# All gate/up chunks of an encoder's feed-forward by seven products, with the two half-token products of a chunk run ahead of its other five

## The chip, the cores and the metric

The kernel runs on one core of one Trainium2 chip. The metric is the device time of one execution in microseconds (us); the comparison is of medians of several executions. The engines are named as in the profile: PE is TensorE's matmul, PEld its weight load, DVE the vector engine, ACT the scalar engine, POOL GpSimd, SP the engine that issues most transfers.

## What is computed

A two-layer bidirectional encoder on 512 tokens of width 1024, everything in float32. Each layer mixes tokens (attention heads and a short convolution side by side) and then runs a gated feed-forward of hidden width 2816:

```
for l in range(DEPTH):                                   # DEPTH = 2
    h = rms_norm(x, pre_mix_norm[l])
    ... attention heads and convolution -> merged ...
    mix = einsum('bse,ed->bsd', merged, w_out[l])
    x = x + rms_norm(mix, post_mix_norm[l])
    h = rms_norm(x, pre_ffn_norm[l])
    g, u = split(einsum('bsd,df->bsf', h, w_gate_up[l]), 2, axis=-1)
    f = einsum('bsf,fd->bsd', silu(g) * u, w_down[l])
    x = x + rms_norm(f, post_ffn_norm[l])
```

The change is in the line of `g, u`: a product of [512 x 1024] by [1024 x 5632].

## The kernel before

**Precision.** Every float32 operand A of a matmul is split into a high part (`hi`, A rounded to TensorE's fast float32 form, a cast on ACT) and a low part (`lo` = A - hi, a subtraction on DVE), and a product is three matmuls: hi*hi, hi*lo, lo*hi. So each block of 128 x 1024 weights costs a cast and a subtraction, beside its matmuls.

**Tiles.** Tokens are in four tiles of 128 (t = 0..3), the width 1024 in eight blocks of 128 (four make a group g = 0, 1). `hT[k][g]` holds the transposed, normalized activations: k = 0 high, k = 1 low, [128, 4, 512 tokens] each. `transposed(t, ...)` (lines 237 to 248) fills one token tile: eight transposes on PE into two PSUM banks, a cast on ACT (L245), a subtraction on DVE (L246), and for the feed-forward a plain copy on ACT (L248) into `raw`. The hidden width is 22 chunks (m = 0..21) of 128 gate and 128 up columns. A chunk's weights come as two transfers of 512 KB (`load_raw`, three buffers tagged `raw`), and are split in halves (`split_half`, L177 on ACT and L178 on DVE) into four buffers `wh`/`wl`.

**A chunk in the direct way** (`pair_full`, m = 0 to 3 before): 2 outputs x 8 blocks x 3 = 48 matmuls with 512 tokens as the moving side; m = 0 and 1 run in two halves of 256 tokens (2 x 48 matmuls), since the token tiles 2 and 3 are not there yet when gate/up starts.

**A chunk by seven products** (`seven`, m = 4 to 21 before): a scheme of Strassen's kind on the 2 x 2 blocks (gate/up columns by width groups on one side, width groups by token halves on the other). Each product is 4 blocks x 3 = 12 matmuls with 256 tokens, so a chunk is 84 of these. It needs sums of token halves (`make_sums`, once per layer, from `raw`: four sums, each then split in high and low) and, for each chunk, four sums of weight blocks (`prepare`: t1 to t4 by four subtractions on DVE, then the splits of t1, t2, of t3, t4 and of the plain blocks b11, b21, b22). Five products use the token sums or the second token half. Two (b11 and b21) use only the first 256 tokens: product b11 by `hT` group 0 and product b21 by group 1, one after the other into the same bank `x`, which after both holds the gate of the first 256 tokens and after the first starts the bank `y`.

**Order.** PE and SP run in the order in which the program writes their instructions (`manual_schedule`). ACT and DVE are put in order at compile time by a planner that goes by its own costs, and takes, of the instructions that it thinks are ready, the one that the program writes first. Each engine then runs its list in that fixed order and waits where an operand is not there.

**Around the change.** In `out_proj`, for each token tile t, the mix is read out of PSUM (`evac`, L660 to L664), its norm is worked out (`rsqrt_mean`), x is updated (`residual`, L629), and the tile is normalized for the feed-forward (`normed`, L232 to L234); tiles 0 and 1 are transposed inside `out_proj`, tiles 2 and 3 inside the first chunks of gate/up. After gate/up come the 22 x 2 blocks of the down product, whose operands are split by `split` (L693, L694).

Of the kernel before, what the change touches and what calls it, by code (L numbers as in the profile page):

```python
# [16 lines left out]
F32 = mybir.dt.float32  # L17
# [6 lines left out]
P = 128  # L24
# [16 lines left out]
NDIRECT = 2  # L41

SEVEN = 4
# [34 lines left out]
def encoder(ctx: ExitStack, tc: tile.TileContext, x, xT, pos, mask, cols, rows, w, out):  # L78
# [32 lines left out]
    def load_raw(i, c=0, d=1024):  # L111

        if i >= 2 * DEPTH * NCHUNK:
            return
# [7 lines left out]
    x_sb = [cpool.tile([P, D], F32, tag=f"x{t}", name=f"x{t}") for t in range(NT)]  # L122
# [45 lines left out]

    def split_half(i):
# [8 lines left out]
        nc.vector.tensor_sub(lo, raws[i], hi.bitcast(F32))  # L178

# [451 lines left out]
    def out_proj(l, merged, sq_a, sq_c, inv):  # L631
# [40 lines left out]
        for t in range(NT):  # L672
# [5 lines left out]
            hs[t] = normed(t, gffn)  # L678
        return hT, hs, raw

    def feed_forward(l, hT, hs, raw):
# [9 lines left out]
        def split(m, src):  # L691
            hi, lo = act_dst(m)
            nc.scalar.copy(hi, src)  # L693
            nc.vector.tensor_sub(lo, src, hi.bitcast(F32))  # L694

        def unsplit(m):

            i = m - NDIRECT
            if i < 8:
                key, make, k = i // 4, lambda: big([P, 4, S]), i % 4  # L700
            elif i < 12:
                key, make, k = i // 2, lambda: sb.tile([P, 2, S], F32, tag="gain", bufs=2, name=nm("gain")), i % 2
            elif i < 18:
                key, make, k = i // 2, lambda: mid([P, 2, S]), i % 2
            else:
                key, k = i, 0
                make = lambda: sb.tile([P, 1, S], F32, tag="u" if i == 18 else "sqa", bufs=1, name=nm("u"))
# [3 lines left out]

        def gated(m, gate, up):

            if m < NDIRECT:
                nc.vector.tensor_mul(gate, up, gate)
                split(m, gate)
            else:
                nc.vector.tensor_mul(unsplit(m), up, gate)

        def gated_full(m, accs):  # L720
            sg = tmp([P, S])
            nc.scalar.activation(sg, accs[0], AF.Silu)
            gated(m, sg, accs[1])

        def turning(t):
            n = [0]

            def step():
                n[0] += 1
                if n[0] == TURN_GU:  # L730
                    transposed(t, hs[t], hT, "att", raw)
            return step
# [6 lines left out]
        def quarter(tiles, g, f):  # L739
            return tiles[g][:, :, f * HS:f * HS + HS]  # L740

        def make_sums():
            a11, a12, a21, a22 = (quarter(raw, g, f) for g, f in ((0, 0), (1, 0), (0, 1), (1, 1)))
            for o, x, y, op, g, f in ((a22, a21, a22, ALU.add, 1, 1), (a21, a11, a21, ALU.subtract, 0, 1),
                                      (a11, a22, a11, ALU.subtract, 0, 0), (a12, a12, a11, ALU.subtract, 1, 0)):
                nc.vector.tensor_tensor(o, x, y, op)
                yield
# [3 lines left out]
                hi = quarter(sums[0], g, f)  # L751
                nc.scalar.copy(hi, o)
                yield
                nc.vector.tensor_sub(quarter(sums[1], g, f), o, hi.bitcast(F32))
                yield

        def split_pair(src, n=1024):
            hi = sb.tile([P, 1024], F32R, tag="wh", bufs=WBUFS, name=nm("wh"))
            lo = sb.tile([P, 1024], F32R, tag="wl", bufs=WBUFS, name=nm("wl"))
            for c in range(0, n, 512):  # L760
                nc.scalar.copy(hi[:, c:c + 512], src[:, c:c + 512])  # L761
            nc.vector.tensor_sub(lo[:, :n], src[:, :n], hi[:, :n].bitcast(F32))  # L762
            return [(hi[:, c:c + 512], lo[:, c:c + 512]) for c in range(0, n, 512)]

        made = {}

        def prepare(m):
# [4 lines left out]
            b1, b2 = raws[i], raws[i + 1]  # L772
            (b11, b12), (b21, b22) = ((b[:, :512], b[:, 512:]) for b in (b1, b2))
            t12 = sb.tile([P, 1024], F32, tag="kl", bufs=2, name=nm("t"))
            t34 = sb.tile([P, 1024], F32, tag="kl", bufs=2, name=nm("t"))
            load_raw(i + 2)
            ops["b11"], = split_pair(b1, 512)
# [4 lines left out]
            load_raw(i + 3)  # L782
            yield
            ops["t1"], ops["t2"] = split_pair(t12)
            yield
            nc.vector.tensor_sub(t34[:, 512:], b21, t12[:, 512:])
            yield
            ops["b21"], ops["b22"] = split_pair(b2)
            yield
            ops["t3"], ops["t4"] = split_pair(t34)  # L790
            yield

        def down_splits():
            for k in (0, None, 1, None, 2, None):
                if k is not None:
                    split_half(2 * (l * NCHUNK + 38) + k)
                yield

        def seven(m, y, ahead):


            ops = made.pop(m)
            x, q = bank("acc"), bank("acc")

            def product(o, weights, tiles, g, f, start):
                hi, lo = weights
                a, b = quarter(tiles[0], g, f), quarter(tiles[1], g, f)
                for k in range(4):
                    c = slice(k * P, k * P + P)
# [225 lines left out]
```

## Time and profile before

| | us |
|---|---|
| median of 3 executions | 1184.53 (1184.43 to 1184.53) |
| profiled execution, device time | 1181.35 |
| its span, first to last instruction | 1179.6 |
| PE busy | 1161.3 (98%) |
| DVE busy | 788.5 (67%) |
| ACT busy | 628.4 (53%) |
| gate/up of layer 0, first matmul to first matmul of down | 236.28 to 468.72 |

The span begins with the first instruction. "Busy" of PE includes the overlap of neighbouring matmuls, so the start-to-start distance of matmuls is the better measure of its work. A timeline row gives the start, the duration, the engine, the line, the operation, the output and inputs, and in brackets how long the engine sat idle before it and which instruction ended that. Durations of neighbours on ACT and DVE overlap by some hundredths of a microsecond too: the start-to-start distance is what one costs in a full queue. The two layers have the same pattern; layer 1 is shifted by 584.40 us.

### The profile page before, as it was taken

To read this page: it belongs to the slowest core of one execution; us is meant where nothing else is said; L and a number is where in the kernel's file an instruction comes from. 1 tells how busy PE (TensorE), PEld (TensorE's weight loads), DVE (VectorE), ACT (ScalarE), POOL (GpSimd) and SP (SyncE) were. 2 spreads that over 40 slices of the span, in tenths; PEclk is the share of its full clock that TensorE was granted. 3 is DMA by queue.
4 is the path that set the end of the run, shared out by engine and by line. 5 is a ranking of instruction groups with operands and counts; after the bars stand their busy time and mean duration, and the time that the engine had idled before them with its cause. 6 is when DMAs were issued, how large, how long until landed. Compare 5 with 4: busy or idle time off the path is not lost.

```text
span 1179.6 us, 17833 instructions
## 1 busy us (share of the span) xinstructions
PE 1161.3 (98%) x7000; PEld 1018.9 (86%) x7000; DVE 788.5 (67%) x1330; ACT 628.4 (53%) x1217; POOL 33.8 (3%) x55
## 2 busy tenths in 40 slices
PE   9999999989999999999999999999999999999997
PEld 7777778888999999888877777788899999998886
DVE  4798655786888888432557986458868888883323
ACT  7577544663565557331445775437636555582311
POOL 5000001000000000000000000100000000000000
PEclk9999999999999999999999999999999999999999
DMA  8221123123333333423132211322223333333221
GB/s 320 90 72 54 55 66 112 56 98 99 107 99 103 106 107 110 158 74 114 46 117 80 72 54 57 99 95 72 79 90 103 106 108 108 108 126 123 91 72 72
DMA packets 33205, 114.38 MB, mean 97 GB/s; under 512 B 3936, under 2 KB 3936, under 8 KB 33120
## 3 DMA queue, kind: packets, MB, share of 16 engines
q1 hardware_dynamic: 32400, 112.15, 29.1%
q8 instruction: 55, 0.90, 0.3%
q10 hardware_dynamic: 720, 1.09, 0.2%
q14 instruction: 30, 0.25, 0.1%
HBM read 111.12 MB, written 2.10 MB: 96 GB/s over the span
## 4 chain that ended last, share of the span: by engine, by line
PE 92%; DVE 4%; ACT 2%; issue 1%; DMA 0%; DVEq 0%; SPq 0%
PE acc L811 18%; PE att L811 13%; PE acc L190 13%; PE acc L192 13%; PE acc L191 13%; PE att L190 4%; PE att L192 4%; PE att L191 4%; PE pv L427 3%; PE att L420 2%; PE att L403 1%; PE att L404 1%; ACT mid L232 1%; PE pv L192 1%; PE pv L190 1%
## 5 line engine op out<-in xcount | busy, mean ns | idle before, releaser
L178 DVE TENSOR_TENSOR wl<-raw,wh 128x1024 fp32r<-128x1024 f32 x120 | 146.5, 1222 | 165.5 <-ACT wh L177 164.9
L177 ACT CAST wh<-raw 128x1024 fp32r<-128x1024 f32 x120 | 125.7, 1050 | 177.7 <-PE acc L192 67.4
L811 PE MATMUL acc<-big,wh 128*128 128x256 f32 x1152 | 212.0, 283 | 0.0
L190 PE MATMUL acc<-big,wh 128*128 128x512 f32 (+1 forms) x496 | 184.8, 372 | 0.0
L191 PE MATMUL acc<-big,wh 128*128 128x512 f32 (+1 forms) x496 | 180.1, 363 | 1.1 <-DVE big L246 1.1
L192 PE MATMUL acc<-big,wl 128*128 128x512 f32 (+1 forms) x496 | 180.1, 363 | 0.0
L811 PEld LDWEIGHTS acc<-big,wh 128*128 128x128 f32 x1152 | 179.8, 192 | 0.2
L811 PE MATMUL acc<-big,wl 128*128 128x256 f32 x576 | 163.0, 283 | 0.0
L811 PE MATMUL att<-big,wh 128*128 128x256 f32 x864 | 160.4, 283 | 0.0
L811 PEld LDWEIGHTS att<-big,wh 128*128 128x128 f32 x864 | 134.7, 192 | 0.2
L811 PE MATMUL att<-big,wl 128*128 128x256 f32 x432 | 122.3, 283 | 0.0
L762 DVE TENSOR_TENSOR wl<-t,wh 128x1024 fp32r<-128x1024 f32 x72 | 88.0, 1223 | 43.0 <-ACT wh L761 43.0
L761 ACT CAST wh<-t 128x512 fp32r<-128x512 f32 x144 | 88.7, 619 | 45.9 <-PE att L811 31.7
L811 PEld LDWEIGHTS acc<-big,wl 128*128 128x128 f32 x576 | 110.6, 192 | 0.0
L192 PEld LDWEIGHTS acc<-big,wl 128*128 128x128 f32 x496 | 93.6, 189 | 15.2
L190 PE MATMUL acc<-wh,big 128*128 128x512 f32 x272 | 106.4, 391 | 0.2 <-ACT wh L524 0.2
L191 PEld LDWEIGHTS acc<-big,wh 128*128 128x128 f32 x496 | 93.8, 189 | 14.5 <-DVE big L246 1.7
L191 PE MATMUL acc<-wl,big 128*128 128x512 f32 x272 | 106.1, 390 | 0.2 <-DVE wl L525 0.2
L192 PE MATMUL acc<-wh,big 128*128 128x512 f32 x272 | 105.9, 389 | 0.0
L190 PEld LDWEIGHTS acc<-big,wh 128*128 128x128 f32 x496 | 93.7, 189 | 13.7 <-issue 0.8
L190 PE MATMUL att<-wh,big 128*128 128x512 f32 x228 | 89.4, 392 | 0.0
L761 ACT CAST wh<-raw 128x512 fp32r<-128x512 f32 x108 | 63.4, 619 | 48.5 <-PE acc L811 31.3
(212 smaller groups left out, 1942.9 us busy)
## 6 DMA issues: line engine op xcount, KB each, us to landing
raw<-in_w SPq DMA_DIRECT2D x192, 512.0 KB, 3.7
gain<-in_rows SPq DMA_DIRECT2D x7, 512.0 KB, 5.6
big<-in_xT SPq DMA_DIRECT2D x8, 256.0 KB, 5.5
raw<-in_w SPq DMA_DIRECT2D x8, 256.0 KB, 5.5
x<-in_x SPq DMA_DIRECT2D x4, 512.0 KB, 7.0
out_dram<-x SPq DMA_DIRECT2D x4, 256.0 KB, 2.1
out_dram<-x ACTq DMA_DIRECT2D x4, 256.0 KB, 2.1
mask_sb<-in_mask SPq DMA_DIRECT2D x1, 448.0 KB, 7.7
```

The lines of the kernel that those rows point to most:

```text
L177: nc.scalar.copy(hi, raws[i])
L178: nc.vector.tensor_sub(lo, raws[i], hi.bitcast(F32))
L190: nc.tensor.matmul(o, sh, mh, start=start, stop=False)
L191: nc.tensor.matmul(o, sh, ml, start=False, stop=False)
L192: nc.tensor.matmul(o, sl, mh, start=False, stop=stop)
L232: nc.scalar.activation(h[:, c], x_sb[t][:, c], AF.Square, accum_out=ss[:, f:f + 1])
L403: nc.tensor.matmul(sc, qk[:, hd, q0:q0 + P], qk[:, 2 + hd, :], start=True, stop=False)
L420: nc.tensor.transpose(tp[:, k * P:(k + 1) * P], sm[:, k * P:(k + 1) * P], ident)
L427: nc.tensor.matmul(o[hd * 64:hd * 64 + 64, half * 256:half * 256 + 256], V[:, k, hc:hc + 64], PT[hd][:, k, :], start=k == 0, stop=k == NT - 1)
L761: nc.scalar.copy(hi[:, c:c + 512], src[:, c:c + 512])
L762: nc.vector.tensor_sub(lo[:, :n], src[:, :n], hi[:, :n].bitcast(F32))
L811: nc.tensor.matmul(o[:, :HS], sh[:, c], mh[:, k, :], start=start and k == 0 and n == 0, stop=k == 3 and n == 2, skip_group_check=True)
```

## The change

All 22 chunks go by seven products. The order of the seven is changed: the two that need only the first half of the tokens (now called the lead of a chunk, `lead1` and `lead2`) are run ahead of the other five (`rest`). The first six leads of a layer (`LEAD` = 6) run one after another at the start of gate/up, each pair with a product of a neighbouring chunk in between, because the second adds to the bank that ACT reads after the first. Token tile 2 is transposed after the second lead's first product, token tile 3 after the fifth's, and each is followed by its part of the token sums (`make_sums(j)`, now by blocks of 128 tokens). The remaining 16 leads are spread over the 22 `rest`s, one in each of 16 of them. The first product of a lead leaves its result in the place where the chunk's output will stand (`unsplit`), from which the `rest` copies it into `y`. The last product (t4) of a chunk moves into the next chunk's `rest`, behind t2.

Lead weights are loaded apart (two transfers of 256 KB, the blocks b11 and b21), and split apart; the `rest` loads the whole chunk again for the four sums and b22. For the buffers of the leads from chunk 6 on, the four tiles of x (512 KB each) are written to DRAM by transfers of the POOL queue after `normed`, and read back after gate/up. Results of gate/up are all kept unsplit until the down product.

```diff
-NDIRECT = 2
-SEVEN = 4
+LEAD = 6
+TURN_LEAD = {1: 2, 4: 3}
...
     def split_half(i):
-        if i >= 2 * DEPTH * NCHUNK or i in halves or SEVEN <= i // 2 % NCHUNK - 16 < MT:
+        if i >= 2 * DEPTH * NCHUNK or i in halves:
             return
-        for k in range(i, min(i + RAW_AHEAD, 2 * DEPTH * NCHUNK - 1) + 1):
-            if k not in raws:
-                load_raw(k)
+        for k in range(i, i + RAW_AHEAD + 1):
+            load_ahead(k)
+        r = gate_half(i)
+        if r is not None:
+            if r < LEAD:
+                split_lead(i // (2 * NCHUNK), r)
+            return
...
+    def load_lead(l, m):
+        if (l, m) in lead_raws:
+            return
+        if m < LEAD:
+            r = sb.tile([P, 1024], F32, tag="raw", bufs=RAW_AHEAD + 1, name=nm("raw"))
+        else:
+            r = sb.tile([P, D], F32, tag="x", bufs=4, name=nm("raw"))
+        lead_raws[l, m] = r
+        for k in range(2):
+            nc.sync.dma_start(r[:, k * 512:k * 512 + 512], w[l * NCHUNK + 16 + m][:, k * 1024:k * 1024 + 512])
+
+    def split_lead(l, m):
+        if (l, m) not in leads:
+            leads[l, m] = split_pair(lead_raws[l, m], 1024, ("wh", "wl") if m < LEAD else ("x", "x"))
...
             hs[t] = normed(t, gffn)
+            nc.gpsimd.dma_start(x_away[:, t, :], x_sb[t])
...
-        def make_sums():
-            a11, a12, a21, a22 = (quarter(raw, g, f) for g, f in ((0, 0), (1, 0), (0, 1), (1, 1)))
+        def make_sums(j):
+            part = [[quarter(raw, g, f, j * P, P) for f in range(2)] for g in range(2)]
+            (a11, a21), (a12, a22) = part
             for o, x, y, op, g, f in ((a22, a21, a22, ALU.add, 1, 1), (a21, a11, a21, ALU.subtract, 0, 1),
                                       (a11, a22, a11, ALU.subtract, 0, 0), (a12, a12, a11, ALU.subtract, 1, 0)):
                 nc.vector.tensor_tensor(o, x, y, op)
+            for o, g, f in ((a22, 1, 1), (a11, 0, 0), (a21, 0, 1), (a12, 1, 0)):
...
-                hi = quarter(sums[0], g, f)
+                hi = quarter(sums[0], g, f, j * P, P)
                 nc.scalar.copy(hi, o)
-                nc.vector.tensor_sub(quarter(sums[1], g, f), o, hi.bitcast(F32))
+                nc.vector.tensor_sub(quarter(sums[1], g, f, j * P, P), o, hi.bitcast(F32))
...
         def prepare(m):
...
             nc.vector.tensor_sub(t12[:, :512], b12, b11)
             nc.vector.tensor_sub(t12[:, 512:], b22, t12[:, :512])
             yield
             nc.vector.tensor_sub(t34[:, :512], b22, b12)
+            load_rest(m + 1, 1)
+            nc.vector.tensor_sub(t34[:, 512:], b21, t12[:, 512:])
             ops["t1"], ops["t2"] = split_pair(t12)
             yield
             ops["t3"], ops["t4"] = split_pair(t34)
             yield
+            ops["b22"], = split_pair(b22, 512)
+            yield
...
+        def lead1(m):
+            x = firsts[m] = bank("acc")
+            product(x, leads[l, m][0], hT, 0, 0, True)
+            nc.scalar.copy(unsplit(m)[:, HS:], x[:, :HS])
+
+        def lead2(m):
+            x = firsts.pop(m)
+            product(x, leads[l, m][1], hT, 1, 0, False)
+            nc.scalar.activation(unsplit(m)[:, :HS], x[:, :HS], AF.Copy if m < LEAD else AF.Silu)
+
+        def last_product(m, y, up):
+            place = unsplit(m)
+            product(y, made.pop(m)["t4"], hT, 1, 1, False)
+            if m < LEAD:
+                nc.scalar.activation(place[:, :HS], place[:, :HS], AF.Silu)
+            nc.scalar.activation(place[:, HS:], y[:, :HS], AF.Silu)
+            nc.vector.tensor_mul(place, up, place)
+
+        def rest(m, y, before, ahead, led):
+            ops = made[m]
+            q = bank("acc")
             up = tmp([P, S])
             p5 = row([P, HS])
+            nc.scalar.copy(y[:, :HS], unsplit(m)[:, HS:])
             product(q, ops["t1"], sums, 1, 1, True)
             nc.scalar.copy(p5, q[:, :HS])
             next(ahead)
             product(y, ops["t2"], sums, 0, 0, False)
             nc.scalar.copy(up[:, :HS], y[:, :HS])
             next(ahead)
+            if before is not None:
+                last_product(*before)
             next(ahead)
+            if led is not None:
+                lead1(led)
             product(y, ops["t3"], sums, 0, 1, False)
             nc.scalar.copy(up[:, HS:], y[:, :HS])
+            nc.vector.tensor_add(up[:, HS:], up[:, HS:], p5)
             product(q, ops["b22"], sums, 1, 0, False)
             nc.vector.tensor_add(up[:, :HS], q[:, :HS], up[:, :HS])
+            if led is not None:
+                lead2(led)
             next(ahead)
+            return m, y, up
...
         ahead = None
+        for m in range(LEAD):
+            for k in range(m, min(m + 3, LEAD)):
+                load_lead(l, k)
+                split_lead(l, k)
+            if m + 3 < LEAD:
+                load_lead(l, m + 3)
+            lead1(m)
+            if m in TURN_LEAD:
+                t = TURN_LEAD[m]
+                transposed(t, hs[t], hT, "att", raw)
+            if m > 0:
+                lead2(m - 1)
+            if m in TURN_LEAD:
+                make_sums(t - 2)
+            if m == LEAD - 3:
+                ahead = prepare(0)
+            if ahead is not None:
+                next(ahead)
+        lead2(LEAD - 1)
         next(ahead)
...
+        led = LEAD
+        load_lead(l, led)
+        split_lead(l, led)
+        load_lead(l, led + 1)
+        before = None
+        for m in range(MT):
+            with_lead = led < MT and led < LEAD + (m + 1) * (MT - LEAD) // (MT - 1)
+            before = rest(m, ys[m % 2], before, prepare(m + 1) if m + 1 < MT else down_splits(),
+                          led if with_lead else None)
+            if with_lead:
+                led += 1
+                if led < MT:
+                    split_lead(l, led)
+                if led + 1 < MT:
+                    load_lead(l, led + 1)
+        last_product(*before)
+        for t in range(NT):
+            x_sb[t] = sb.tile([P, D], F32, tag="x", bufs=4, name=nm("x"))
+            nc.gpsimd.dma_start(x_sb[t], x_away[:, t, :])
```

More of the change, by code (lines that the diff above doesn't have):

```diff
@@ L750, in make_sums, with load_rest @@
                         sums[k][g] = big([P, 4, S], F32R)
-                hi = quarter(sums[0], g, f)
+                hi = quarter(sums[0], g, f, j * P, P)
                 nc.scalar.copy(hi, o)
-                yield
-                nc.vector.tensor_sub(quarter(sums[1], g, f), o, hi.bitcast(F32))
[L755 to L763, printed above, removed]
+                nc.vector.tensor_sub(quarter(sums[1], g, f, j * P, P), o, hi.bitcast(F32))
         made = {}
+        def load_rest(m, h):
+            if m < MT and 2 * (base + m) + h not in raws:
+                load_raw(2 * (base + m) + h)
         def prepare(m):
@@ L791, in prepare @@
             yield
[L793 to L809, printed above, removed]
-                    for n, (sh, mh) in enumerate(((hi, a), (hi, b), (lo, a))):
-                        nc.tensor.matmul(o[:, :HS], sh[:, c], mh[:, k, :], start=start and k == 0 and n == 0,
-                                         stop=k == 3 and n == 2, skip_group_check=True)
-            hA = [[hT[k][g] for g in range(2)] for k in range(2)]
+            ops["b22"], = split_pair(b22, 512)
@@ new lines, in prepare, with product @@
+            yield
+        def product(o, weights, tiles, g, f, start):
+            hi, lo = weights
+            a, b = quarter(tiles[0], g, f), quarter(tiles[1], g, f)
+            for k in range(4):
+                c = slice(k * P, k * P + P)
+                for n, (sh, mh) in enumerate(((hi, a), (hi, b), (lo, a))):
+                    nc.tensor.matmul(o[:, :HS], sh[:, c], mh[:, k, :], start=start and k == 0 and n == 0,
+                                     stop=k == 3 and n == 2, skip_group_check=True)
@@ L815, in seven @@
+        def rest(m, y, before, ahead, led):
+            ops = made[m]
+            q = bank("acc")
             up = tmp([P, S])
-            gate = tmp([P, S])
             p5 = row([P, HS])
-            product(x, ops["b11"], hA[0:2], 0, 0, True)
-            nc.scalar.copy(y[:, :HS], x[:, :HS])
-            next(ahead)
+            nc.scalar.copy(y[:, :HS], unsplit(m)[:, HS:])
             product(q, ops["t1"], sums, 1, 1, True)
@@ L887, in feed_forward @@
         hs = [None] * NT
-        done = set()
+        done = set(range(4))
         def down(f, m, t, acc, keep=None):
-            if m >= NDIRECT and m not in done:
-                split(m, unsplit(m))
+            if m not in done:
+                split(m)
             done.add(m)
@@ L913, in feed_forward @@
                     for k in range(m, min(m + 4, MT)):
-                        if k >= NDIRECT and k not in done:
-                            split(k, unsplit(k))
+                        if k not in done:
+                            split(k)
                             done.add(k)
-                    if m == 14 - 3:
+                    if m == 18 - 3:
                         gpost = load_row(l, 3)
```

128 lines of the change are left out of this document (47 added, 81 removed).

## The prediction, made before the changed kernel was run

> **What bounds the kernel now.** I read the page first, for the engine on which the end hangs.
>
> ```profile
> PE 1161.3 (98%) x7000; PEld 1018.9 (86%) x7000; DVE 788.5 (67%) x1330; ACT 628.4 (53%) x1217; POOL 33.8 (3%) x55
> ...
> PE 92%; DVE 4%; ACT 2%; issue 1%; DMA 0%; DVEq 0%; SPq 0%
> ```
>
> PE is busy for 98% of the span, and 92% of the chain of waits is PE. So a change pays by fewer or cheaper matmuls, as long as nobody makes PE wait. The next question is what stands still in the stage that is changed. The table of stretches (length in us, busy time of PE, PEld, DVE, ACT, POOL with instruction counts, granted clock, DMA share, GB/s) gives, for layer 0, the first four chunks and then the eighteen that already go by seven products:
>
> ```profile
> 236.28:287.29 51.01, 47.62 (x309) 43.33 (x308) 38.52 (x58) 27.02 (x50) 0.00 (x0) 1.00 0.31 103
> 287.29:468.73 181.44, 181.44 (x1514) 181.34 (x1513) 145.94 (x198) 110.22 (x239) 0.00 (x0) 1.00 0.33 105
> ```
>
> In the second stretch PE never stops. In the first it stands 51.01 - 47.62 = 3.39 us, and the waits of PE between 236 and 288 name them (engine, line, releaser, us, times, longest):
>
> ```profile
> PE att L241 <- DVE small L213: 2.8, 1, 2.8
> PE acc L191 <- DVE big L246: 0.5, 1, 0.5
> ```
>
> L241 is the transposing of token tile 2. It waits for DVE. How full DVE is there, the stretches show:
>
> ```profile
> 236.00:246.00 10.00, 6.61 (x52) 6.08 (x52) 9.93 (x22) 6.74 (x17) 0.00 (x0) 1.00 0.62 206
> 258.00:269.00 11.00, 11.00 (x78) 10.28 (x77) 10.97 (x12) 8.73 (x11) 0.00 (x0) 1.00 0.28 97
> 269.00:287.29 18.29, 18.29 (x83) 15.18 (x82) 9.59 (x13) 4.49 (x9) 0.00 (x0) 1.00 0.36 115
> ```
>
> DVE is full until 246 and again from 258 to 269 (tail of the output projection, then token sums and weight splits), and only then has slack. The four direct chunks are what gives it that time. This is the place where the change presses.
>
> **The change, part by part.** *Matmuls saved.* Start-to-start distances on PE (timeline rows; the two rows of the chain of waits are 84 matmuls apart):
>
> ```profile
> 236.28 0.28 PE L190 MATMUL acc<-big,wh 128*128 128x256 f32 x1
> 237.32 0.28 PE L192 MATMUL acc<-big,wl 128*128 128x256 f32 x1
> 237.44 0.28 PE L190 MATMUL acc<-big,wh 128*128 128x256 f32 x1
> 244.40 1.06 PE L241 MATMUL att<-ident,mid 128*128 128x128 f32 x8 [2.85 <-DVE small L213]
> 245.22 0.36 PE L190 MATMUL acc<-big,wh 128*128 128x256 f32 x1
> ...
> 287.29 2.87 PE acc L811 x24
> 297.37 2.88 PE acc L811 x24
> ...
> 275.32 0.60 ACT L722 ACTIVATE tmp<-acc 128x512 f32<-128x512 f32 x1 [4.32 <-PE acc L192]
> 286.20 0.60 ACT L722 ACTIVATE tmp<-acc 128x512 f32<-128x512 f32 x1 [3.80 <-PE acc L192]
> ...
> 468.72 0.40 PE L190 MATMUL acc<-wh,big 128*128 128x512 f32 x1
> ```
>
> A 256-token matmul costs 0.120 us (237.44 - 237.32), a chunk by seven products 297.37 - 287.29 = 10.08 us = 84 x 0.120, one product of twelve 1.44 us. A direct chunk costs 286.20 - 275.32 = 10.88 us, and one run in two token halves 96 x 0.120 = 11.52 us. The four direct chunks of a layer cost 2 x 11.52 + 2 x 10.88 = 44.80 us and become 40.32 us: 4.48 us less PE work a layer.
>
> The Trainium skill (TensorE: Matmul & The Clock Gate, "Wait — 56ns, not 53.3ns?") puts matmuls at N / 2.4 GHz plus about 2.5 ns, measured there on bf16: 109 ns for 256 columns and 216 for 512, by which the saving would be about 5.0 us a layer, an estimate. The trace has 120 ns and 10.88 / 48 = 227 ns, so it disagrees by some 11 ns on each, and the rows decide.
>
> *What DVE must do first.* Product t1 of a chunk needs split weight sums, and from the first chunk on it needs the token sums of all tiles. Before, the first such product ran at 287.29. Now it is the thirteenth product. I count it from where DVE has finished with the last token tile's normalization. The rows (DVE timeline; neighbours give what an instruction takes in a full queue):
>
> ```profile
> 249.10 1.28 DVE L234 SCALAR_TENSOR_TENSOR mid<-x,small,gain 128x1024 f32<-128x1024 f32 x1
> 252.32 1.29 DVE L246 TENSOR_TENSOR big<-att,big 128x512 fp32r<-128x512 f32 x2 [1.93 <-ACT big L245]
> ...
> 257.80 1.22 DVE L178 TENSOR_TENSOR wl<-raw,wh 128x1024 fp32r<-128x1024 f32 x1
> 258.94 2.48 DVE L746 TENSOR_TENSOR big<-big,big 128x1024 f32<-128x1024 f32 x2
> ...
> 273.16 0.69 DVE L781 TENSOR_TENSOR t<-raw,raw 128x512 f32<-128x512 f32 x1
> 273.76 0.68 DVE L786 TENSOR_TENSOR t<-raw,t 128x512 f32<-128x512 f32 x1
> ...
> 295.61 0.42 DVE L834 TENSOR_TENSOR tmp<-tmp,row 128x256 f32<-128x256 f32 x1
> 295.96 0.42 DVE L833 TENSOR_TENSOR tmp<-acc,tmp 128x256 f32<-128x256 f32 x1
> ```
>
> A subtraction of 1024 elements costs 258.94 - 257.80 = 1.14 us, one of 512 elements 0.60 (273.76 - 273.16), one of 256 0.35. L234 ends its share at 249.10 + 1.20 = 250.3. Up to there the work is the same as before, instruction for instruction (two lead splits of 1024 elements stand for two half-chunk splits). From 250.3 on, until PE can run t1 of chunk 1, the program has DVE do:
>
> - leads 4, 5 and 6, low parts: 3 x 1.14 = 3.42
> - token tile 3, low parts: 2 x 0.60 = 1.20
> - token sums in blocks of 512 elements: 2 tiles x (4 sums + 4 low parts) x 0.60 = 9.60
> - chunk 0: four weight sums 2.40, low parts of t1/t2 and t3/t4 2.28, of b22 0.60, together 5.28
> - chunk 1: four weight sums 2.40, low part of t1/t2 1.14, together 3.54
>
> The sum is 23.0 us, so t1 of chunk 1 starts at about 250.3 + 23.0 = 273.3. PE by itself would be there earlier: from the transposing at 244.40, which ends at 245.22, fourteen more products (20.2), the other transposing (0.8) and two opening matmuls (0.5) lead to 266.7. Leads, token sums and chunk 0 each hold PE up somewhere; the sum of the waits is what counts, and DVE sets it. Behind that point PE has 154 - 16 = 138 products: 138 x 1.44 = 198.7 us, less the 0.24 us by which a product may start before its low part. Down then starts at 273.3 + 198.7 - 0.2 = 471.8, against 468.72 before: **3.1 us later a layer**, though PE has less to do.
>
> *Order.* DVE's fixed order also has to wait for others. The nearest row is the 1.93 us in front of L246 above, in a queue with less to choose from. Below, a luckier order gains (a rival, worked out there); above, twice that wait is 3.9 us a layer. With 23 us queued up there is nearly always something ready, so I take 0.4 and have **3.5 us a layer, 7.0 in all**.
>
> *ACT.* Its casts cost 0.52 (two in 1.14), its 256-element copies about 0.28 by spacing and 0.37 alone:
>
> ```profile
> 248.39 0.23 ACT L210 ACTIVATE small<-small 128x1 f32<-128x1 f32 x1
> 275.81 1.14 ACT L761 CAST wh<-t 128x512 fp32r<-128x512 f32 x2
> 290.20 0.37 ACT L822 COPY row<-acc 128x256 f32<-128x256 f32 x1 [0.62 <-PE acc L811]
> ```
>
> From 248.6 to t1 of chunk 1 it has some 23 casts (leads, token sums, chunks 0 and 1) at 0.52, four copies at about 0.5 for tile 3, and 14 copies of 0.28: 18 us, done near 267. It is ahead of DVE, so nothing is added; if its copies came last behind casts, one lead product could wait 0.5 us, inside the order term.
>
> *Afterwards.* With a lead, a chunk costs DVE 2.40 + 2.28 + 0.60 + 1.14 + 2 x 0.35 + 0.60 = 7.7 us against 10.08 on PE; without one, 6.6 against 7.2. So DVE recovers, and the 138 products run without gaps. One chain is tight: b22's split can take its buffer only after t4 of the chunk before, and in the five later `rest`s without a lead only t3 (1.44 + 0.24) covers a cast, a subtraction and the hand-overs (0.62 + 0.69 + about 0.15 = 1.5). I take 0; two copies ahead of that cast would make it 0.3 late, 1.7 us a layer.
>
> *Transfers.* By the page:
>
> ```profile
> raw<-in_w SPq DMA_DIRECT2D x192, 512.0 KB, 3.7
> out_dram<-x SPq DMA_DIRECT2D x4, 256.0 KB, 2.1
> ```
>
> Leads add 11 MB of loads over some 220 us and four tiles of x out and back (2 MB each way), to a DMA share of 0.31 to 0.33. SP's order has each lead load a whole chunk (7 us or more) ahead of its split. The x tiles come back some 60 us before the second half of down needs them. POOL computes nothing in this stage. Its transfers appear in no row; at twice the 2.1 us of the nearest, tile 3's store lands near 255, before lead 7 wants that buffer (262). I add 0; a late lead load would cost at most one landing, 3.7 us, and mostly inside the wait for DVE.
>
> *Sum.* The profiled execution took 1181.35 us (span 1179.6): 1181.35 + 7.0 = 1188.4. The median of the runs lies 3.2 us above that execution, so I put the same change on it: 1184.5 + 7.0 = **1191.5 us**.
>
> **The rivals.** *The clock falls in a wait.* PE's waits in a layer come to about 12 us (t1 of chunk 1 at 273.3, less 236.28 and 25.1 us of work: 16 products, two transposings, two opening matmuls), so one may be longer than the 2.85 us seen. The granted clock is the third column from the right:
>
> ```profile
> 241.00:245.00 4.00, 1.15 (x11) 0.98 (x10) 3.93 (x10) 0.94 (x4) 0.00 (x0) 1.00 0.69 204
> ...
> 1173.00:1174.00 1.00, 0.00 (x0) 0.00 (x0) 0.25 (x1) 0.93 (x3) 0.00 (x0) 1.00 0.06 18
> 1175.00:1176.00 1.00, 0.00 (x0) 0.00 (x0) 0.96 (x3) 0.00 (x0) 0.00 (x0) 0.56 0.00 0
> ```
>
> It stayed at 1.00 over the wait of 2.85 us, and fell to half about 2 us after PE's last matmul at the end (0.56 in the second from 1175), so a wait of 3 to 5 us can meet it. A few us at half speed, say 3.4 to 6.8 a layer, would cost 1.7 to 3.4 us a layer: 1195 to 1198. The Trainium skill (same page, Part 1) has the clock halved after an idle window of about 3.4 us and restored after about 3.4 us of work, which speaks against a change that trades matmuls for waits; the single price by it is about 1.7 us per fall.
>
> *The order on DVE is better than the program's.* Low parts of tokens (2.4 us; needed first by t4), lead 6 (1.14) and two weight sums of chunk 1 (1.2) may come after t1 of chunk 1, which then starts at 273.3 - 4.7 = 268.6. The next bound is b22 of chunk 1: DVE is there at 273.3 + 1.14 + 0.60 + 0.70 = 275.7, with 133 products (191.5) to go: down at 467.0, **1.7 us earlier a layer**, 1181.1 in all. For it speaks that the planner has let weight splits (L178) pass other work before; against it, that it takes the earlier written first when both are ready, and that a perfect order is needed.
>
> *DVE doesn't bind.* Then only the wait for token tile 2 grows: its transposing now stands behind 24 matmuls of gate/up, not 36, so 1.44 us more, 4.48 - 1.44 = 3.0 us gained a layer: 1178.4. Against it stand 38.52 busy us of DVE in 51 us before. It would need my count of 23 us to be a third too high.
>
> That the change doesn't do what it says I exclude: 22 chunks x 84 matmuls x 2 layers are written out.
>
> **How the numbers follow.** The forecast has 0.55, the fallen clock 0.15, the better order (or a way to it that ends near no change) 0.23, no bound by DVE 0.07. A measurement of this kernel can tell about 0.2%, 2.4 us, from no change: 1182.1 to 1186.9. Slower takes the fallen clock and nearly all of the forecast: 0.67. Same takes most of the third case and the forecast's lower edge: 0.20. Faster takes the rest: 0.13. The range for 8 in 10 goes from the better order's 1181 to 1201, which holds the upper order term (7.0 a layer, 1198.5) and a clock that falls on top; the forecast's own range is 1187 to 1196.
>
> **What would show it.** The first five-product `rest` starts near 262 to 267 and t1 of chunk 1 near 273 in layer 0; PE's waits in the first 37 us of gate/up rise from 3.4 to about 12 us and name low parts made by DVE (or its casts); DVE has no idle time there; from chunk 2 on PE doesn't stop; down starts near 472. I am wrong if down starts before 468.7, if PE waits further on in the stage, or if a transfer ends a wait.

## The result and the profile after

| | before | after |
|---|---|---|
| median | 1184.53 us (1184.43 to 1184.54, 4 runs) | 1198.09 us (1194.99 to 1199.69, 4 runs) |
| ratio | | 1.0112, 95% interval 1.0088 to 1.0135 |
| profiled execution, span | 1181.35, 1179.6 us | 1194.99, 1193.0 us |
| gate/up, first matmul to first of down, layer 0 | 232.4 us | 238.4 us |
| the same, layer 1 | 232.4 us | 240.0 us |

The change makes the kernel slower by 13.6 us, nearly twice the 7.0 us of the forecast: inside the range for 8 in 10 (1181 to 1201 us), above the forecast's own (1187 to 1196). Nearly all of it lies in gate/up: 5.9 us in layer 0 (238.36 - 232.44) and 7.5 us in layer 1 (239.96 - 232.43). (Line numbers are those of the changed kernel: products are at L819 in place of L811, transposing at L286, DVE's low parts of weights at L222, its weight sums at L800 to L805, the cast of a token sum at L780.)

The page, busy times and the chain of waits:

```profile
PE 1161.3 (97%) x7096; PEld 1023.7 (86%) x7096; DVE 815.9 (68%) x1410; ACT 662.0 (55%) x1361; POOL 43.9 (4%) x71
...
PE 87%; DVE 6%; DMA 3%; ACT 3%; issue 1%; DVEq 0%; SPq 0%; ACTq 0%
```

PE is busy as long as before, although it has 9 us less to do, and its share of the chain has gone from 92% to 87%. The time has become waits, and slow matmuls. PE's waits by releaser, both layers (us in all, times, longest):

```profile
PE att L286 <- DVE small L258: 9.9, 2, 5.0
PE acc L819 <- DVE wl L222: 4.3, 2, 2.2
PE att L819 <- ACT tmp L857: 2.9, 5, 1.7
```

PE's timeline in layer 0, the rows with a wait, and the first row of down:

```profile
237.00 0.39 PE L819 MATMUL acc<-big,wh 128*128 128x256 f32 x1 [0.53 <-DVE big L291]
244.98 1.94 PE L286 MATMUL att<-ident,mid 128*128 128x128 f32 x8 [4.98 <-DVE small L258]
264.90 0.38 PE L819 MATMUL acc<-big,wh 128*128 128x256 f32 x1 [0.49 <-DVE big L781]
267.31 0.39 PE L819 MATMUL att<-big,wh 128*128 128x256 f32 x1 [0.51 <-DVE big L781]
269.44 0.50 PE L819 MATMUL att<-big,wh 128*128 128x256 f32 x2 [0.55 <-ACT tmp L857]
275.00 0.39 PE L819 MATMUL acc<-big,wl 128*128 128x256 f32 x1 [2.19 <-DVE wl L222]
...
474.55 0.40 PE L235 MATMUL acc<-wh,big 128*128 128x512 f32 x1
```

The wait at 275.00 is that of t1 of chunk 1 for its low part, which the forecast put at 273.3. The wait for token tile 2 grew from 2.85 to 4.98 us, and behind it the eight transposes took 1.94 us, not 1.06. The stretches say why (third column from the right: granted clock):

```profile
241.00:245.00 4.00, 0.02 (x1) 0.05 (x1) 3.75 (x9) 1.87 (x9) 0.00 (x0) 0.84 0.59 179
245.00:248.50 3.50, 3.50 (x17) 3.50 (x18) 2.36 (x6) 2.29 (x6) 0.53 (x1) 0.50 0.48 180
248.50:252.00 3.50, 3.50 (x24) 3.50 (x23) 3.32 (x8) 3.18 (x9) 0.00 (x0) 0.70 0.23 90
...
246.00:266.00 20.00, 19.51 (x145) 19.14 (x144) 18.68 (x32) 19.37 (x46) 0.53 (x1) 0.89 0.43 138
252.00:275.00 23.00, 19.26 (x152) 18.15 (x151) 22.96 (x35) 21.25 (x48) 0.00 (x0) 1.00 0.51 155
```

The clock fell to half during the wait (0.84 means 1.3 us at half, so from 243.7) and came back at about 250.6: PE worked 5.6 us at half speed, which is 2.8 us of PE's time lost. From 252 to 275 DVE is busy for 22.96 of 23 us. ACT, which the forecast had well ahead, is busy for 19.37 of 20 us from 246 to 266.

### The profile page after: what moved, and what is told of

Same layout as the page of the kernel before. It is cut to its first block, busy times and chain, and to the rows that moved or that the text cites. A ratio compares the mean times of both kernels' runs of the same rounds, so it can differ in the third digit from the quotient of the medians.

```text
span 1193.0 us, 18412 instructions
## 1 busy us (share of the span) xinstructions
PE 1161.3 (97%) x7096; PEld 1023.7 (86%) x7096; DVE 815.9 (68%) x1410; ACT 662.0 (55%) x1361; POOL 43.9 (4%) x71
## 4 chain that ended last, share of the span: by engine, by line
PE 87%; DVE 6%; DMA 3%; ACT 3%; issue 1%; DVEq 0%; SPq 0%; ACTq 0%
PE acc L819 18%; PE att L819 15%; PE acc L235 10%; PE acc L237 10%; PE acc L236 10%; PE att L235 4%; PE att L236 4%; PE att L237 4%; DMA raw<-in_w 3%; PE pv L472 3%; PE att L465 2%; PE att L448 1%; PE att L449 1%; DVE wl L222 1%; PE pv L235 1%
## 5 line engine op out<-in xcount | busy, mean ns | idle before, releaser
L819 PE MATMUL att<-big,wh 128*128 128x256 f32 x1056 | 195.5, 284 | 4.1 <-ACT tmp L857 2.9
L819 PE MATMUL acc<-big,wh 128*128 128x256 f32 x896 | 169.7, 288 | 1.9 <-DVE big L291 1.1
L819 PEld LDWEIGHTS att<-big,wh 128*128 128x128 f32 x1056 | 164.6, 192 | 6.5 <-ACT tmp L857 4.5
L222 DVE TENSOR_TENSOR wl<-t,wh 128x1024 fp32r<-128x1024 f32 x88 | 107.4, 1222 | 66.8 <-ACT wh L221 63.1
L819 PE MATMUL att<-big,wl 128*128 128x256 f32 x528 | 149.4, 283 | 0.0
L819 PEld LDWEIGHTS acc<-big,wh 128*128 128x128 f32 x896 | 143.0, 196 | 3.3 <-DVE big L291 1.7
L819 PE MATMUL acc<-big,wl 128*128 128x256 f32 x448 | 128.5, 287 | 4.3 <-DVE wl L222 4.3
L235 PE MATMUL acc<-big,wh 128*128 128x512 f32 x304 | 123.3, 406 | 0.0
L237 PE MATMUL acc<-big,wl 128*128 128x512 f32 x304 | 119.1, 392 | 0.0
L236 PE MATMUL acc<-big,wh 128*128 128x512 f32 x304 | 118.7, 391 | 0.0
L819 PE MATMUL acc<-big,x 128*128 128x256 f32 x768 | 102.6, 283 | 0.0
L819 PEld LDWEIGHTS att<-big,wl 128*128 128x128 f32 x528 | 101.3, 192 | 0.0
L819 PEld LDWEIGHTS acc<-big,x 128*128 128x128 f32 x768 | 96.8, 192 | 0.0
L819 PEld LDWEIGHTS acc<-big,wl 128*128 128x128 f32 x448 | 87.6, 195 | 4.7 <-DVE wl L222 4.7
L235 PE MATMUL att<-wh,big 128*128 128x512 f32 x228 | 89.4, 392 | 0.0
L237 PE MATMUL att<-wh,big 128*128 128x512 f32 x228 | 88.8, 389 | 0.0
```

What stands on the lines that cost most here:

```text
L235: nc.tensor.matmul(o, sh, mh, start=start, stop=False)
L236: nc.tensor.matmul(o, sh, ml, start=False, stop=False)
L237: nc.tensor.matmul(o, sl, mh, start=False, stop=stop)
L819: nc.tensor.matmul(o[:, :HS], sh[:, c], mh[:, k, :], start=start and k == 0 and n == 0, stop=k == 3 and n == 2, skip_group_check=True)
```

## The experiments

Ratios are to the kernel before, run on the same chip in the same series; the kernel before took 1183.0 us (15 runs) beside e1 to e4, 1184.1 us (15 runs) beside the changed kernel's second run and e5 to e7, and 1183.2 us (12 runs) beside e8 and e9. The changed kernel itself ran only in the first comparison (1.0112) and beside e5 to e7 (1.0128), so the others are set against both ratios.

| kernel | median us | ratio, 95% interval |
|---|---|---|
| changed kernel, second run | 1198.68 | 1.0128 (1.0113 to 1.0144) |
| e1: idle matmuls in the wait for tile 2 | 1195.31 | 1.0104 (1.0085 to 1.0123) |
| e2: no low parts of token sums | 1193.58 | 1.0094 (1.0075 to 1.0114) |
| e3: token sums on POOL | 1209.79 | 1.0226 (1.0207 to 1.0244) |
| e4: before, one more chunk by seven products | 1181.61 | 0.9986 (0.9974 to 0.9997) |
| e5: no token sums at all | 1189.75 | 1.0050 (1.0037 to 1.0064) |
| e6: ten leads | 1204.01 | 1.0170 (1.0156 to 1.0184) |
| e7: before, idle matmuls in the wait for tile 2 | 1181.47 | 0.9980 (0.9971 to 0.9988) |
| e8: e4 and e7 together | 1180.06 | 0.9971 (0.9961 to 0.9981) |
| e9: ten leads, results in other buffers | 1190.63 | 1.0067 (1.0050 to 1.0085) |

**The clock: e1.** The theory on record was V (DVE's queue sets the time), the rival C (the fallen clock).

```diff
+                if t == 2:
+                    b = bank("pv")
+                    for _ in range(32):
+                        nc.tensor.matmul(b[:, :HS], hT[0][0][:, 0, :P], hT[0][0][:, 0, :HS], start=True, stop=True)
                 transposed(t, hs[t], hT, "att", raw)
```

> The changed kernel with 32 idle matmuls of 256 columns (3.8 us, into a bank that nobody reads) in PE's list ahead of the transposing of token tile 2, so that PE's wait of 4.98 us there shrinks to about 1.1 us and the granted clock should stay at 1.00. Theory V (DVE's queue sets when t1 of chunk 1 can start): PE's speed ahead of that point hardly matters, since DVE has no gap there that PE causes; 0 to 1 us less a layer, 1196 to 1198 us. Theory C (the fallen clock is what was missing in the forecast): the 5.6 us of matmuls at half speed come back, 2.8 us a layer, 1192.5 us, and the spread between executions (1195.0 to 1199.7) shrinks.

It took 1195.31 us, between V's 1196 and C's 1192.5, nearer to V; the spread stayed (1193.3 to 1197.0). PE's rows in layer 0, and two later stretches:

```profile
245.28 1.06 PE L286 MATMUL att<-ident,mid 128*128 128x128 f32 x8 [1.12 <-DVE small L258]
274.51 0.39 PE L819 MATMUL acc<-big,wl 128*128 128x256 f32 x1 [2.17 <-DVE wl L222]
...
264.00:276.00 12.00, 8.31 (x57) 7.58 (x58) 11.90 (x18) 8.86 (x20) 0.00 (x0) 0.96 0.49 162
276.00:290.00 14.00, 14.00 (x110) 14.00 (x109) 10.46 (x16) 5.85 (x14) 0.00 (x0) 0.91 0.38 120
```

The transposes ran at full speed (1.06 us) and PE did its leads sooner, but t1 of chunk 1 still waited 2.17 us for its low part, and started only 0.8 us earlier against the stage's beginning than in the changed kernel (38.0 us after it; before that 38.8). DVE is full (11.90 of 12 us), and the clock now fell in the later waits. So the speed of PE ahead of that point matters little, as V has it, but a fall behind it costs in its own right. Layer 1 of this run says it best: its clock stayed at 1.00 from the first matmul of gate/up to the first of down, and it still took 238.57 us, 6.1 us more than before (232.43).

```profile
827.70:1066.27 238.57, 230.90 (x1900) 228.24 (x1899) 197.75 (x294) 154.05 (x357) 3.24 (x6) 1.00 0.49 161
```

One reservation: with more instructions on PE the planner also ordered DVE a little differently.

**DVE, and ACT behind it: e2 and e5.** e2 takes 4.8 us a layer off DVE, e5 9.6 us off DVE and 4.2 us off ACT. Both matmul with the plain tokens in place.

```diff
+                sums[1][g] = hT[1][g]                                                           # e2
...
-                nc.vector.tensor_sub(quarter(sums[1], g, f, j * P, P), o, hi.bitcast(F32))      # e2
...
+            for g in range(2):
+                sums[0][g], sums[1][g] = hT[0][g], hT[1][g]                                     # e5
+            return
```

> The changed kernel without the low parts of the token sums: DVE's eight subtractions of 512 elements a layer are left out, and the matmuls take the low parts of the plain tokens in their place, so PE does the same work on other numbers (the output is not the reference's). Theory V: DVE has 8 x 0.60 = 4.8 us less ahead of t1 of chunk 1 and PE gets there as much earlier: 9.6 us in all, about 1188.5 us. Theory C (clock) or a bound by transfers: no change, 1197 to 1198 us.

e2 gave 1.0094, where 1.0128 or 1.0112 was the changed kernel's: 2 to 4 us won of the 9.6 that V expected. V in this form is wrong. Its PE timeline and waits show who stands there instead:

```profile
PE att L818 <- ACT big L780: 5.1, 2, 3.1
...
268.31 0.68 PE L818 MATMUL att<-big,wh 128*128 128x256 f32 x2 [1.99 <-ACT big L780]
```

L780 is ACT's cast of a token sum: what PE now waits for is made by ACT. (The profiled execution is the slowest of the four, 1196.64 us. The clock fell a second time behind this wait, to 0.57 from 268 to 272, which eats a part of what DVE gave.) ACT was as full as DVE, so I went on with theory VA: both queues are full, ACT close behind DVE.

> The changed kernel without the token sums: the eight sums of a layer, their eight casts and eight low parts are left out, and the matmuls take the plain token halves in their place (the output is not the reference's; PE's work is the same). DVE is rid of 16 x 0.60 = 9.6 us a layer, ACT of 8 x 0.52 = 4.2 us. Theory VA (both queues are full up to t1 of chunk 1, ACT close behind DVE, which is why the lows alone gave little): the gain is ACT's 4.2 us a layer, some 8 us in all, 1.002 to 1.005 of the kernel before. Theory V (DVE alone): up to 6.6 us a layer, where PE by itself is the bound, at or below the kernel before, 0.998 to 1.000. Theory C (clock): nothing changes, since the wait for tile 2 stays, 1.010.

e5 came to 1.0050: 9 us less than the changed kernel beside it (1198.68 - 1189.75), at the edge of what VA expects (1.002 to 1.005), above V's 0.998 to 1.000 and below C's 1.010. The wait for a low part of weights (L222) is gone from PE's list. In layer 0, t2 of chunk 1 starts 37.6 us after the stage's beginning, against 40.1 in the changed kernel's first profile and 41.4 in its second, where the clock had fallen just before. Against full clock that is 2.5 us, so the total's match with ACT's 4.2 us a layer is no proof. The stretch behind the slow matmuls shows what bounds this run:

```profile
252.00:272.00 20.00, 18.28 (x150) 17.79 (x149) 14.62 (x19) 17.31 (x40) 0.00 (x0) 1.00 0.56 185
```

Neither DVE (14.62 of 20 us) nor ACT (17.31) is full, and PE (18.28) is the busiest. What is left stands ahead of it: the wait of 5.0 us for token tile 2 and 6 us of matmuls at half speed, which V's "PE by itself" did not count; copies of ACT still end waits of up to 1.5 us. So e5 shows that the token sums on the two queues are worth some 9 us, but it can't tell V from VA; that ACT is the next bound rests on the wait in e2.

**Moving the sums: e3.**

```diff
-                nc.vector.tensor_tensor(o, x, y, op)
+                nc.gpsimd.tensor_tensor(o, x, y, op)
```

> The changed kernel with the eight token sums of a layer (512 elements each) on POOL in place of DVE. POOL's 512-element additions took 1.4 us in the kernel before, so the four of a token tile take about 5.6 us in a row, beside DVE. Theory V: DVE is rid of 4.8 us; the sums of tile 3 come some 3 us later than DVE would make them, so 3 to 4.8 us a layer are won, 1188.5 to 1192 us. If POOL's additions slow DVE down while they run, less. Theory C: no change, 1197 to 1198 us.

It missed by far: 1.0226, some 12 to 13.5 us slower than the changed kernel. The timelines of POOL, ACT and PE:

```profile
266.91 1.62 POOL L774 TENSOR_TENSOR big<-big 128x512 f32<-128x512 f32 x1
...
270.25 0.62 ACT L780 CAST big<-big 128x512 fp32r<-128x512 f32 x1 [1.07 <-POOL big L774]
271.92 0.62 ACT L780 CAST big<-big 128x512 fp32r<-128x512 f32 x1 [1.05 <-POOL big L774]
275.05 0.38 ACT L852 COPY att<-big 128x256 f32<-128x256 f32 x1
...
275.49 0.80 PE L819 MATMUL att<-big,wh 128*128 128x256 f32 x2 [4.79 <-ACT att L852]
```

A sum took 1.3 to 2.2 us on POOL, mostly more than the 1.4 us I took from the kernel before, and ACT's list has the four casts in a row: each stands until POOL has the next sum, and behind them stands L852, the copy that PE waits 4.79 us for. An engine that is spared work wins nothing if another, full one then waits in order for the slower helper.

**What the matmuls alone are worth: e4.**

```diff
-SEVEN = 4
+SEVEN = 3
```

> The kernel before with only one more chunk by seven products (chunks 3 to 21, no leads, no transfers of x): the plain saving of matmuls. One direct chunk of 10.88 us becomes 10.08 us a layer: 1.6 us in all, 1182.9 us, if DVE has the time (it has 8.7 idle us in the last 18 us of that stage). If DVE doesn't have it, 1184.5 to 1187 us.

0.9986 is some 1.6 us less, as expected, though the interval (0.4 to 3.1 us) would allow half or twice of it. The rows of e7 and e8 below, whose clock stayed full, settle it: they differ by this one chunk, and gate/up takes 232.42 us in layer 0 of e7 and 231.63 in e8, 0.8 us less. Where DVE has the time, the saving arrives in full.

**More cover: e6 and e9.** The changed kernel again beside them, for its clock:

> The changed kernel again, beside the next three on one chip, as their measure. On the chip of the first comparison it took 1.0112 of the kernel before; with executions of the kernel before that spread from 1181 to 1188 us on another chip, 1.009 to 1.013 is expected. Its time less what the granted clock cost (span x (1 - mean clock)) was 1187.3 us, and should be that again within 1 us, if the spread is the clock's.

It took 1198.68 us; less span x (1 - mean clock) this is 1187.9 us, as expected. e6 puts more products ahead of the five-product part:

```diff
-LEAD = 6
-TURN_LEAD = {1: 2, 4: 3}
+LEAD = 10
+TURN_LEAD = {3: 2, 6: 3}
```

> The changed kernel with ten leads at the start of gate/up in place of six, and token tile 2 transposed after the fourth lead's first product, tile 3 after the seventh's: no work is added or left out. Eight products (11.5 us of PE) more stand ahead of t1 of chunk 0, for 4 x 1.14 us more of DVE and about 4 x 1.6 us more of ACT ahead of it; and the wait for tile 2 (4.98 us) is covered by four more products (5.8 us). Theory VA: 5 to 7 us less a layer, about the time of the kernel before, 0.998 to 1.003. Theory C: only what the wait for tile 2 cost, 2 to 3 us a layer, 1.006 to 1.008.

It missed too: 1.0170. The wait for tile 2 is gone, but PE and ACT have these rows:

```profile
271.74 0.80 PE L819 MATMUL acc<-big,wh 128*128 128x256 f32 x2 [9.46 <-ACT big L830]
...
270.71 0.62 ACT L780 CAST big<-big 128x512 fp32r<-128x512 f32 x1 [0.58 <-DVE big L774]
271.31 0.65 ACT L830 COPY big<-acc 128x256 f32<-128x256 f32 x2
```

L830 copies the result of a lead's first product to its place. It stood until the last cast of a token sum was done. The program says why: of the eleven big buffers, four hold the tokens, four the token sums, two the raw tokens and one the results of chunks 0 to 3; the results of chunks 6 to 13 go into those of the raw tokens, which are free only after the token sums. With six leads nothing has to go there so early. e9 gives chunks 6 to 9 the two gain buffers:

```diff
-            elif m < 14:
+            elif m < 10:
+                key, make, k = m // 2 + 20, lambda: sb.tile([P, 2, S], F32, tag="gain", bufs=2, name=nm("gain")), m % 2
+            elif m < 18:
                 key, make, k = (m + 2) // 4 + 10, lambda: big([P, 4, S]), (m + 2) % 4
-            elif m < 18:
-                key, make, k = m // 2 + 20, lambda: sb.tile([P, 2, S], F32, tag="gain", bufs=2, name=nm("gain")), m % 2
```

> The changed kernel with ten leads at the start and tiles 2 and 3 transposed after the fourth and the seventh, as in the run with ten leads, but the results of chunks 6 to 9 kept in the two row buffers (gain) that are free by then, and those of chunks 10 to 17 in the two big buffers of the raw tokens, which are free only after the token sums. No work is added or left out. Theory VA (the full queues of DVE and ACT ahead of the five-product part set the time, and more leads cover them): the wait of 9.5 us on the copy of a lead's result is gone, and the time is 5 to 7 us a layer under the changed kernel: 0.999 to 1.004 of the kernel before. If the ten-lead run was slow for another reason than the place of the results, it stays near 1.017.

1.0067: the wait of 9.5 us is gone, and it is the fastest of the changed kernels that leave no work out, 5 to 7 us under the changed one (1.0112 and 1.0128). It is short of the 10 to 14 us that VA expected, and lies in the 1.006 to 1.008 that theory C had for ten leads in e6's expectation. It is still slower than before. PE's waits and the stretch of the first chunks' five-product parts:

```profile
PE acc L819 <- DVE wl L222: 5.7, 4, 2.6
PE att L819 <- ACT tmp L857: 5.5, 6, 3.0
...
272.00:282.00 10.00, 5.72 (x44) 5.23 (x43) 9.24 (x14) 8.36 (x21) 0.00 (x0) 1.00 0.70 243
```

The press on the two queues is put off, from 264 to 275 to 272 to 282. It isn't shown to be smaller: the waits for L222 and L857 are longer than in the changed kernel (4.3 and 2.9 us), and PE's waits in layer 0 add up to 9.1 us, against 9.5 in its first profile. What is gone is the 5.6 us of matmuls at half speed: the clock stayed at 1.00 in layer 0, which took 235.97 us against 238.36. More leads cover the wait for tile 2 and with it the fall, not the queues.

**The clock in the kernel before: e7, and the version that is fastest: e8.**

```diff
                 if n[0] == TURN_GU:
+                    if t == 2:
+                        b = bank("pv")
+                        for _ in range(20):
+                            nc.tensor.matmul(b[:, :HS], hT[0][0][:, 0, :P], hT[0][0][:, 0, :HS], start=True, stop=True)
                     transposed(t, hs[t], hT, "att", raw)
```

> The kernel before with 20 idle matmuls of 256 columns (2.4 us) ahead of the transposing of token tile 2, where PE waited for 2.85 us: nothing else changes, the lists of DVE and ACT are the same. If it is the clock that spreads the kernel before from 1181 to 1188 us (its time less the clock's cost, span x (1 - mean clock), was 1179.3 us within 0.5), the spread goes and the time is that of its fastest executions, 1181 us, 0.998. If the spread has another cause, 1183 us, 1.000.

Right on both counts: 1181.47 us, 11 runs from 1181.23 to 1181.86, where the kernel before beside it took 1182.76 to 1186.0. ACT's and DVE's lists are the same there, so it is the clock alone. The fall itself can be seen in e4's profiled execution, which has the same wait (transposes at half speed, then the stretch):

```profile
244.35 1.94 PE L241 MATMUL att<-ident,mid 128*128 128x128 f32 x8 [2.85 <-DVE small L213]
...
244.00:248.00 4.00, 3.65 (x20) 3.68 (x21) 3.49 (x10) 2.53 (x7) 0.00 (x0) 0.60 0.37 129
```

> The kernel before with both small gains: chunk 3 by seven products too (1.6 us less PE work, measured 0.9986 alone), and 20 idle matmuls ahead of the transposing of token tile 2 (measured 0.998 alone, the spread gone). If the two are independent, 0.9965 of the kernel before, 1180 us, with a spread under 1 us. If DVE cannot give chunk 3's split any earlier once PE runs at full clock, no better than 0.998.

1180.06 us (1179.63 to 1180.62), 0.9971: 3.1 us under the kernel before, faster than both kernels. The two gains nearly add up (0.9986 x 0.9980 = 0.9966).

## Why the prediction was right, and where it was off

*The place and the sign were right.* "DVE is full until 246 and again from 258 to 269 ... This is the place where the change presses." In the changed kernel DVE has no gap but one of 1.11 us from 246 to 275, and nearly all the loss is in gate/up. DVE's rows at the two ends of the sum, and the gap:

```profile
247.71 0.69 DVE L800 TENSOR_TENSOR t<-raw 128x512 f32<-128x512 f32 x1 [1.11 <-DMA raw<-in_w]
250.41 1.28 DVE L279 SCALAR_TENSOR_TENSOR mid<-x,small,gain 128x1024 f32<-128x1024 f32 x1
273.72 2.36 DVE L222 TENSOR_TENSOR wl<-t,wh 128x1024 fp32r<-128x1024 f32 x2
```

*The sum of DVE's work was right, with some luck.* It said 23.0 us from the last token tile's normalization to the low part of t1 of chunk 1. That is 250.41 + 1.20 = 251.6 to 273.72 + 1.14 = 274.9: 23.3 us. Two differences cancel in it: the first weight sum of chunk 0 (0.60) was already done, and two additions of chunk 0's output (0.70), which the sum did not have, stand in its place. *Its start was 1.3 us late* (251.6, not 250.3): that weight sum stood in DVE's list ahead of the normalization and waited 1.11 us for its transfer, and tile 2's normalization already came 0.6 us later (243.55, not 242.98); a wait of 0.79 us that the kernel before had there fell away. The step "the same as before, instruction for instruction" left this out. PE lost 13.7 us up to 275.0 (38.8 us less 25.1 of work), where 12 were predicted: 9.3 us of waits, 2.8 us by matmuls at half speed, and 1.6 us that neither covers. More than half of the waits (4.98 us) is for token tile 2, not for low parts, as the prediction had named.

*The ACT step failed.* It had "18 us, done near 267. It is ahead of DVE, so nothing is added". ACT is busy for 19.37 of 20 us from 246 to 266 and goes on to 275, because the planner also puts the table load (1.28 us), the Silu of gates already finished and the copies for chunk 0 there, which I had placed later. For the changed kernel this cost little, since DVE was as late: nothing in layer 0, 0.9 us in layer 1, where DVE waits for casts (rows below) and ACT had itself stood 1.3 us for the weights of a lead. e2 shows that ACT would have been the next bound, which the rivals "the order on DVE is better" and "DVE doesn't bind" did not have.

*The order term was too small.* That late start is such a term, for which I took 0.4 us a layer out of 0 to 3.9: t1 of chunk 1 ran 1.7 us later than 273.3 in layer 0. Counted from the stage's beginning it is 1.8 us late there (38.8 against 37.0) and 2.8 us late in layer 1 (39.8). DVE's waits in layer 1, from 836 to 867, and the row of PE:

```profile
DVE t L800 <- DMA raw<-in_w: 1.1, 1, 1.1
DVE big L781 <- ACT big L780: 0.5, 1, 0.5
DVE wl L222 <- ACT wh L221: 0.4, 1, 0.4
...
866.32 0.39 PE L819 MATMUL acc<-big,wl 128*128 128x256 f32 x1 [2.13 <-DVE wl L222]
```

*"The 138 products run without gaps" was off by 1 to 2 us a layer.* From 275.0 - 0.2 to 474.55 it took 199.8 us, not 198.7, and in layer 1 200.4 us. In three `rest`s without a lead in each layer t3 waited for the copy of t2's result (L857), which sits in ACT's list behind a cast of lead weights; in five of the six that cast stood until the weights had landed. ACT's wait in layer 0 from 275 to 475:

```profile
ACT x L221 <- DMA raw<-in_w: 13.5, 8, 2.5
```

and one such place in the timeline of ACT and PE:

```profile
421.56 0.62 ACT L221 CAST x<-raw 128x512 fp32r<-128x512 f32 x1 [1.65 <-DMA raw<-in_w]
422.09 0.36 ACT L857 COPY tmp<-att 128x256 f32<-128x256 f32 x1
422.11 0.28 PE L819 MATMUL att<-big,wl 128*128 128x256 f32 x1
...
422.51 0.51 PE L819 MATMUL att<-big,wh 128*128 128x256 f32 x2
```

The cast of lead weights stands 1.65 us for its transfer, L857 is queued behind it, and t3 starts 0.40 us after the last matmul of t4 (422.11), where matmuls without a wait follow each other at 0.12.

I had said of transfers "I add 0", and that a transfer that ends a wait would make me wrong: here it does so by way of ACT. The other sign of being wrong, that PE waits further on in the stage, came with it. It wasn't tried how much comes back if the leads land earlier.

*The fallen clock was a rival; it came, but it is not most of what was missing.* I gave it 0.15 and 1195 to 1198 us, and the median is 1198.09, so by the number alone the rival would have won. It fell in the wait of 4.98 us, in both layers. But the rows close the forecast's sum without a term for it: t1 of chunk 1 is 1.8 and 2.8 us late, and the products behind it take 1.1 and 1.7 us more. That is 7.4 us in two layers, less the 0.8 us that the forecast had for order: the missing 6.6 us. Most of PE's slow time lies where PE would have waited for DVE: taking it away, as e1 did, brought t1 of chunk 1 forward by 0.8 us in layer 0 and 1.0 us in layer 1 (38.0 and 38.8 us after the stage's beginning), so the fall has at most some 1.8 us of the 6.6.

Where the clock does cost is behind that point. In the changed kernel's second profiled execution (1198.71 us) it fell again in the wait for t1 of chunk 1, and gate/up took 240.4 and 241.7 us, 2.1 and 1.7 more than in the first (1194.99 us):

```profile
244.00:248.00 4.00, 2.94 (x14) 2.97 (x15) 2.61 (x6) 1.95 (x6) 0.53 (x1) 0.57 0.44 135
...
276.00:280.00 4.00, 4.00 (x26) 4.00 (x25) 3.47 (x6) 0.78 (x2) 0.00 (x0) 0.67 0.41 139
```

The kernel before pays about as much for its own fall (e7 won 2.6 us by filling the wait), and the medians stand 3.1 (after) and 3.2 us (before) above the profiled executions, and the step "I put the same change on it" came out right. That was luck: the forecast had no fall in it, neither that of the kernel before nor one in a later wait of the changed kernel. (The clock's own account, span x (1 - mean clock), has 11.1 us for the changed kernel and 4.5 for the one before. It also counts slow time in which PE would have waited and some 2 us behind PE's last matmul, which cost nothing.)

*Matmuls saved: right.* 0.80 us for a direct chunk agrees with e4 and with the rows of e7 and e8.

## What to carry to other kernels

A saving on the busiest engine is worth what the other engines' queues leave of it at that place: count what each in-order queue must do between the last point that is unchanged and the first instruction that needs its result, and do it for every engine that is nearly full, not only for the one that is named. The direct chunks cost PE 4.48 us a layer more, and paid for it by giving DVE and ACT more than 20 us to get ready. Where a wait cannot be removed, some matmuls without a use in it can be cheaper than the wait alone: 20 of them made the kernel before 2.6 us faster.

## What the runs showed of the hardware

The clock explains nearly all of the spread between executions. In 15 executions of the kernel before, from 1180.97 to 1187.61 us, the mean granted clock went from 0.998 down to 0.993, and time less span x (1 - clock) is 1179.3 us with a deviation of 0.5. A wait of 2.85 us is enough to meet it in some executions: e4's profile shows the fall there, the profile of the kernel before doesn't, and filling 2.4 us of it with idle matmuls (e7) took the range from 3.2 to 0.6 us. In the changed kernel's first profile the clock fell 3.7 us after PE's last matmul (240.0 to 243.7) and came back 5.6 us after PE had begun again: 6.8 us at half in all. In the second, behind the same wait, it was 3.4 us (0.57 over 4.00 us, by the row above), and 3.4 us in e4 too (0.97 from 240 to 244, then 0.60 over 4.00 us). The Trainium skill (TensorE: Matmul & The Clock Gate, Part 1) has windows of about 3.4 us that run freely; the traces agree, with 3.4 and 6.8 us at half, one window and two, and the fall after about 2 us at the end of the kernel and the different executions fit windows that don't start with the wait. That the fall needs an idle window of that whole length, as the prediction took from the page, e4 does not bear out: it came in a wait of 2.85 us. PE worked through 5.6 us of the fall in layer 0 of the first profile and 2.8 us of the second, so its price was 2.8 and 1.4 us, around the 1.7 us that I worked out from that page.

POOL's addition of 128 x 512 float32 took 1.4 us in the kernel before and 1.3 to 2.2 us in e3, where DVE was busy for 21.94 of 25 us beside it (250 to 275); DVE does it in 0.60 us.
